# One product of a fast matrix multiplication by seven instead of whole, with sums moved to GpSimd

## The chip, the cores and the metric

The kernel runs on one core of a Trainium2 chip. The core has TensorE (matrix products, called PE in the profile; its loads of the stationary operand are PEld), VectorE (DVE), ScalarE (ACT), GpSimd (POOL) and SyncE (SP), each with a queue of its own that it works off in order. PSUM has eight banks, each of 128 rows of 512 float32 numbers. TensorE adds its results up there, and VectorE and ScalarE read them. The metric is device time in microseconds, and the median of several runs is given.

## What is computed

```python
x = np.random.randn(8, 2048, 2048).astype(np.float32)
w = np.random.randn(2048, 2048).astype(np.float32)
cs = np.cumsum(x, axis=1)
diff = cs - (cs shifted down by one row, with a row of zeros ahead)
out = np.matmul(diff, w)
```

Taking the differences of a running sum gives `x` back, so the kernel computes `x @ w`: 16384 rows by 2048 by 2048, with float32 in and out.

## The kernel before

**Tiles.** The 16384 rows are 128 tiles of 128 rows. The first four tiles are multiplied in the plain way while the weights arrive. The other 124 form 31 groups of four tiles, `g`, `h`, `k`, `l`. Two groups have orders of their own (`group_plain`, `group_half`); the other 29 are objects of the class `Group`. These 29 are nearly all of the run.

**Seven products for eight.** In a group the four tiles and the weights are cut into 2 x 2 blocks, so that a product of blocks in the plain way takes eight block products. A known scheme (Strassen's, in Winograd's form) takes seven, named `P1` to `P7`, at the price of sums of blocks ahead of them (`S1` to `S4` of the tiles, `T1` to `T4` of the weights) and of sums of the results behind them. The same scheme is used once more inside a product: it is then cut into quarters and done in seven quarters `p1` to `p7` of four matmuls each, instead of eight. Before the change `P1` to `P5` are done so. `P6` (S2 x T2) and `P7` (S3 x T3) are done whole, in 2 x 4 steps of four matmuls each (`whole`).

**Steps of a group.** Each step has a name. `load`, `weigh0`, `weigh1`, `scale`, `unit`, `narrow0`, `narrow1`, `turn0`, `turn1` bring in a tile: SP loads both halves into `F` (line 111), ScalarE takes the sum of magnitudes of each half (`weigh`, line 123), VectorE adds the two and takes the reciprocal (`scale`, lines 139 and 141), GpSimd makes the factor that undoes the scaling (`unit`, line 147), ScalarE scales and narrows to float16 in place (`narrow`, line 158), and SP transposes by DMA into the tile's place (`turn`, line 171). The first halves of the tiles take turns in three places of `F`, the second halves in two.
`P1.s1` to `P1.s4` and the like are the small sums of a product by seven (`small_sums`, VectorE, line 544, 128x512 float16); `S1.g` and the like are the sums on whole blocks (line 544, 128x1024). `P1.fp4` and the like are fills: VectorE writes a sum of weights that has no place of its own into the one tile `flow` (line 937), from which the quarter of that name then reads. The quarters' matmuls have line 573, the whole products' line 554.
`by_seven` lets sums of results form in PSUM: ScalarE copies a bank (`cg`, `ct`, line 1023) and VectorE merges banks (`m1`, `m2`, line 1030). `keep.C11g0` scales a bank into a result tile `c` (ScalarE, line 581), `add.C11g0.v` scales another and adds it (VectorE, line 584), `put.C11g0` stores it (SP, line 595). There are seven `c` tiles; a `put` gives its tile back, and the copies `ct` use them too. Banks and the tiles for small sums are handed out and given back in the same way.

**Order.** `ORDER` is a list of all steps of a group, written out. `P1.p2+1` is the step of the group after the current one, `+0` of the current one, `+2` of the one after the next. One round of the list is done for each group. An engine's instructions are issued strictly in the order of the list (`after`), so a step that waits holds up the steps behind it on its engine. Steps that wait for another engine's result are released by semaphores. The last group's `P4` steps follow in `END_ORDER`.

Of the kernel before, what the change touches and what calls it, by code (L numbers as in the profile page):

```python
# [10 lines left out]
def kernel(  # L11
# [6 lines left out]
    nc = tc.nc  # L18
# [113 lines left out]
    def scale_of(t):  # L132
        if t < END:
# [3 lines left out]
            after(  # L137
                "dve",
                lambda: nc.vector.tensor_scalar(m, m2[:, :1], m2[:, 1:2], TINY, ADD, MAX),  # L139
            )  # L140
            after("dve", lambda: nc.vector.reciprocal(s, m))  # L141
            sizes[t] = m

    def unit_of(t):
        if t < END:
            u, m = unit[t], sizes.pop(t)
            after("pool", lambda: nc.gpsimd.tensor_scalar(u, m, uw, None, MUL))  # L147
# [346 lines left out]
    class Inner:  # L494
# [20 lines left out]
        def weights(self):  # L515
# [4 lines left out]
            return {j: pieces_of(t) for j, t in places.items()}  # L520
# [22 lines left out]
    def total(dst, p, q, op):  # L543
        after("dve", lambda: nc.vector.tensor_tensor(dst.all, p.all, q.all, op))  # L544
# [388 lines left out]

    def fill_by(op, a, b):
        def some():
# [4 lines left out]

    sevens = {
# [8 lines left out]
                "p5": fill_by(SUB, quarter_of(1, 1, 1), quarter_of(6, 1, 0)),  # L950
# [5 lines left out]

    class Group:
        def __init__(self, g):
            self.tiles = dict(g=g, h=g + 2, k=g + 1, l=g + 3)
# [26 lines left out]
        def quarter(self, P, j, b, fresh):  # L986
# [4 lines left out]
            def some():  # L991
                to, a = self.bank(b, fresh), self.sums[P][j]
                quarter(
                    to, self.real(a), passed if j in passes else inner.weights()[j], fresh
                )
# [5 lines left out]
        def small_sums(self, P, a, b, dead, places=()):  # L1001
# [5 lines left out]
            def one(j, p, q, op):  # L1007
                if isinstance(to[j], str):
                    self.take(to[j], scratch)
                total(self.real(to[j]), self.real(p), self.real(q), op)  # L1010
# [48 lines left out]
        def add(self, c, b, tag, let=False):  # L1059
            def some():  # L1060
                add(self.at[c], self.at[b], unit[self.row(c)])
# [4 lines left out]
        def put(self, c):  # L1066
            n = 2 * (c[2] == "2") + int(c[4])
            self.step(f"put.{c}", lambda: put(self.at.pop(c), self.row(c), n))

        def plan(self):  # L1070
            tiles = self.tiles
            half = {}
            for c, t in tiles.items():
# [3 lines left out]
                self.step(f"scale.{c}", scale_of, t)  # L1077
# [74 lines left out]
            self.whole("P7", T3, half["g"][0], half["h"][0], *x)  # L1152
# [43 lines left out]
    put.C12g1+0 turn1.h+1 add.C12h1.q+0 P4.p6+0 P4.p5+0 P1.cg+1 P1.p2+1  # L1196
    add.C12h0.q+0 put.C12h0+0 P1.s1+1 narrow1.k+1 P4.s4+0 P4.p3+0 turn0.k+1
    keep.C21g1+0 P1.s2+1 P1.s4+1 P1.p5+1 add.C22h0.x+0 P1.ct+1 add.C21h1.e+0
# [87 lines left out]
```

## Time and profile before

| | |
|---|---|
| median of 3 runs | 1456.87 us (1456.62 to 1457.39) |
| span of the profiled execution | 1455.0 us |
| TensorE busy | 1441.1 us (99%), 6673 matmuls |
| VectorE busy | 1333.3 us (92%) |
| ScalarE busy | 967.5 us (66%) |
| GpSimd busy | 48.6 us (3%) |
| DMA | mean 242 GB/s |

The profiled execution's own time is its span, 1455.0 us from the first to the last instruction; the runs' times have 1.9 us more around it. In the profile's rows "c<-b,of,c" says that a tile c is written from b, of and c; "x26" is a count; "mean ns" is the mean duration of one. In rows in order of time the first number is the start, the second the duration, both in us, and a bracket at the end tells how long the engine had been idle and what ended that. Neighbours on one engine overlap a little, so what an instruction takes from its engine is read from its start to the next one's.

### The profile page before, as it was taken

The page shows a single profiled execution, that of the slowest core. Times are in us where ns is not written, and L with a number is a line of the kernel's source. Part 1 is how long each engine was busy: PE and PEld are TensorE (multiplying, and loading weights), DVE is VectorE, ACT ScalarE, POOL GpSimd, SP SyncE. Part 2 cuts the span into 40 slices and gives each one's busy share as a digit, 9 for nine tenths or more (in the row PEclk, how much of TensorE's full clock was granted, in tenths as well). Part 3 has the DMA queues.
Part 4 walks back from the last instruction along what each step waited for, and adds up shares of the span by engine and source line. Part 5 has one row for each costly group of instructions (what it writes and reads, how often), then busy time and mean ns, then how long its engine had stood idle before and what let it go on. Part 6 is the DMA issues. An engine that isn't in the chain of part 4 may idle for free.

```text
span 1455.0 us, 20120 instructions
## 1 busy us (share of the span) xinstructions
PE 1441.1 (99%) x6673; PEld 652.6 (45%) x6679; DVE 1333.3 (92%) x2302; ACT 967.5 (66%) x1446; POOL 48.6 (3%) x136
## 2 busy tenths in 40 slices
PE   8999999999999999999999999999999999999998
PEld 3444444444444444444444444444444444444443
DVE  7998899999999999999999999999999999999998
ACT  5887656676666666667666667766666766666662
POOL 0111000000000000000000000000000000000000
PEclk9999999999999999999999999999999999999999
DMA  9999868898888998878998888998878898888983
GB/s 360 367 240 299 236 171 234 248 246 232 234 237 237 248 253 230 235 236 233 260 241 233 231 228 240 260 238 241 225 235 247 247 233 239 226 244 246 253 203 123
DMA packets 377752, 351.59 MB, mean 242 GB/s; under 512 B 274800, under 2 KB 274800, under 8 KB 377520
## 3 DMA queue, kind: packets, MB, share of 16 engines
q1 hardware_dynamic: 377088, 348.47, 84.9%
q0 software_dynamic: 560, 1.84, 0.3%
q8 instruction: 52, 0.85, 0.2%
q14 instruction: 52, 0.43, 0.1%
HBM read 150.99 MB, written 134.22 MB: 196 GB/s over the span
## 4 chain that ended last, share of the span: by engine, by line
PE 96%; DMA 2%; DVE 1%; issue 0%; ACT 0%; SPq 0%; DVEq 0%; ACTq 0%
PE b L573 61%; PE b L554 32%; PE b L275 2%; DMA W<-in_w_dram 1%; DMA W<-in_x_dram 1%; DVE c L584 1%; ACT wb L259 0%; PE b L400 0%; DVE x L544 0%; SPq L219 0%; DVE b L1030 0%; DVE flow L937 0%; DVE inner L544 0%; DVE W L541 0%; ACT c L581 0%
## 5 line engine op out<-in xcount | busy, mean ns | idle before, releaser
L584 DVE SCALAR_TENSOR_TENSOR c<-b,of,c 128x512 f32<-128x512 f32 x790 | 574.1, 747 | 74.3 <-PE b L573 64.3
L554 PE MATMUL b<-W,x 128*128 128x512 f16 x2144 | 506.6, 379 | 0.0
L581 ACT ACTIVATE c<-b,of 128x512 f32<-128x512 f32 x492 | 312.6, 680 | 230.9 <-PE b L573 113.3
L573 PE MATMUL b<-W,x 128*128 128x512 f16 x1892 | 452.4, 379 | 0.8 <-ACT b L1023 0.7
L158 ACT ACTIVATE F<-F,of 128x1024 f16<-128x1024 f32 x246 | 282.2, 1147 | 174.8 <-DVE of L141 172.6
L573 PEld LDWEIGHTS <-x 128*128 128x128 f16 x2488 | 243.4, 98 | 295.3 <-issue 2.7
L554 PEld LDWEIGHTS <-x 128*128 128x128 f16 x2144 | 209.8, 98 | 253.0 <-DVE x L544 0.2
L123 ACT ACTIVATE waste<-F 128x1024 uint8<-128x1024 f32 x246 | 259.3, 1054 | 4.6 <-DMA F<-in_x_dram 2.5
L573 PEld LDWEIGHTS <-inner 128*128 128x128 f16 x1648 | 161.2, 98 | 195.6 <-issue 1.3
L573 PE MATMUL b<-W,inner 128*128 128x512 f16 x944 | 242.2, 379 | 0.9 <-DVE b L1030 0.9
L544 DVE TENSOR_TENSOR x<-x,x 128x1024 f16<-128x1024 f16 (+1 forms) x388 | 226.6, 584 | 3.3
L573 PE MATMUL b<-flow,x 128*128 128x512 f16 x588 | 150.9, 379 | 0.0
L573 PE MATMUL b<-inner 128*128 128x512 f16 x472 | 121.1, 379 | 0.0
L937 DVE TENSOR_TENSOR flow<-W 128x2048 f16<-128x2048 f16 x87 | 105.8, 1216 | 0.0
L1030 DVE TENSOR_TENSOR b<-b,c 128x512 f32<-128x512 f32 x116 | 80.6, 695 | 13.9 <-PE b L573 13.9
L147 POOL TENSOR_SCALAR of<-of,uw 128x1 f32<-128x1 f32 x124 | 43.6, 370 | 1306.7 <-DVE of L139 704.1
L937 DVE TENSOR_TENSOR flow<-W,inner 128x2048 f16<-128x2048 f16 x58 | 70.8, 1220 | 0.0
L1023 ACT COPY c<-b 128x512 f32<-128x512 f32 x58 | 33.4, 576 | 51.3 <-PE b L573 51.3
L275 PE MATMUL b<-wb,xP 128*128 128x512 bf16 x234 | 57.0, 395 | 5.3 <-ACT wb L259 3.9
L544 DVE TENSOR_TENSOR inner<-x 128x512 f16<-128x512 f16 x117 | 49.4, 422 | 2.9 <-DMA x<-F 0.9
L1023 ACT COPY b<-b 128x512 f32<-128x512 f32 x87 | 51.2, 588 | 0.5 <-PE b L573 0.5
L544 DVE TENSOR_TENSOR inner<-x,inner 128x512 f16<-128x512 f16 x117 | 49.2, 421 | 2.0
(67 smaller groups left out, 530.0 us busy)
## 6 DMA issues: line engine op xcount, KB each, us to landing
F<-in_x_dram SPq DMA_DIRECT2D x246, 512.0 KB, 5.1
out_dram<-c SPq DMA_DIRECT2D x492, 256.0 KB, 3.0
W<-in_w_dram SPq DMA_DIRECT2D x32, 512.0 KB, 9.6
W<-in_x_dram SPq DMA_DIRECT2D x16, 256.0 KB, 7.2
x<-F SPq DMA_TRANSPOSE x246, 3.4
out_dram<-o POOLq DMA_DIRECT2D x5, 256.0 KB, 4.1
out_dram<-o SPq DMA_DIRECT2D x5, 256.0 KB, 3.5
xP<-in_x_dram SPq DMA_DIRECT2D x1, 1024.0 KB, 5.1
```

The costliest lines, as they stand in the source:

```text
L123: lambda: nc.scalar.activation(waste, where[t][i], ABS, scale=1.0 / ROW, accum_out=sums_of[t][:, i : i + 1],),
L147: after("pool", lambda: nc.gpsimd.tensor_scalar(u, m, uw, None, MUL))
L158: lambda: nc.scalar.activation(narrowed(t)[:, ds(i * NH, NH)], where[t][i], COPY, scale=s),
L275: lambda: nc.tensor.matmul(ps[r][n], xP[:, r, ko, :], wb[h, ko][:, ds(n * NB, NB)], start=(ko == 0), stop=(ko == KO - 1),),
L544: after("dve", lambda: nc.vector.tensor_tensor(dst.all, p.all, q.all, op))
L554: said = nc.tensor.matmul(to[n], a[k], b[k][:, n, :], start=(first and k == 0), stop=(k == KH - 1), skip_group_check=True,)
L573: said = nc.tensor.matmul(to, a[k], b[k], start=(first and k == 0), stop=(k == 3), skip_group_check=True)
L581: after("act", lambda: nc.scalar.activation(c, p, COPY, scale=u))
L584: after("dve", lambda: nc.vector.scalar_tensor_tensor(c, p, u, c, MUL, ADD))
L937: after("dve", lambda: nc.vector.tensor_tensor(in_twos(flow), x, y, op))
L1023: after("act", lambda: nc.scalar.copy(c, p))
L1030: after("dve", lambda: nc.vector.tensor_tensor(t, p, s, ADD))
```

## The change

It consists of these parts.

- `P7` = S3 x T3 is done in seven quarters in every `Group`, by a new method `onto`. It adds onto four banks that already hold sums: ScalarE copies partial results of two more banks `q` and `e` into `c` tiles (`c1`, `c5`, `c6`, `c7`), and VectorE merges them into the four (`a1`, `a5g`, `a5h`, `a6`, `a7h`, `a7k`). Three of the seven sums of weights come by fills (`fp4`, `fp5`, `fp7`); the quarters of T3 are changed once, ahead of the first group, by two sums.
- From the eleventh tile on, the first halves in `F` take turns in two places. The third holds a sum of weights for `P5`, which so loses the fill `fp5`.
- Nine small sums (`ON_POOL`) and the sum ahead of each reciprocal go to GpSimd. The reciprocal becomes a step `recip`.
- Eight of the sixteen results (`LATE`) are kept by a plain copy and added up without a factor. A step `last` on ScalarE then scales the result in its tile. The last group does as before.
- The order is a new one; each step of the list above that stands in the old order, and is not replaced, stands in the new one, most at another place.

```diff
+    THREE = 11
     for i, t in enumerate(queue_of_x):
-        where[t] = [F[:, i % 3, :], F[:, 3 + i % 2, :]]
+        j = i % 3 if i < THREE else (i - THREE) % 2
+        where[t] = [F[:, j, :], F[:, 3 + i % 2, :]]
...
+    ON_POOL = "P1.s2 P2.s2 P2.s4 P3.s1 P3.s4 P4.s2 P4.s4 P5.s3 P5.s4".split()
+    def total(dst, p, q, op, pool=False):
+        if pool:
+            after("pool", lambda: nc.gpsimd.tensor_tensor(dst.all, p.all, q.all, op))
+        else:
+            after("dve", lambda: nc.vector.tensor_tensor(dst.all, p.all, q.all, op))
...
+    in_5.Q1 = F[:, 2, :].bitcast(f16).rearrange("p (k n) -> p k n", k=4)
+    in_7 = Inner(5, None, quarter_of(5, 0, 1), None)
...
-                "p5": fill_by(SUB, quarter_of(1, 1, 1), quarter_of(6, 1, 0)),
+        "P7": (
+            in_7,
+            {
+                "p4": fill_by(SUB, quarter_of(5, 1, 0), quarter_of(5, 0, 1)),
+                "p5": fill_by(SUB, quarter_of(5, 1, 1), quarter_of(5, 0, 1)),
+                "p7": fill_by(SUB, quarter_of(5, 0, 1), quarter_of(5, 0, 0)),
+            },
+        ),
...
+    LATE = 'C12g0 C12g1 C12h1 C12h0 C11g1 C11h1 C21g1 C21h1'.split()
+            self.late = LATE if g + 4 < END else ()
...
+        def onto(self, P, h0, h1, g0, g1):
+            q, e = f"{P}q", f"{P}e"
+            def snap(name, b, let=False):
+                def some():
+                    c, p = self.take(name, free), self.at[b]
+                    after("act", lambda: nc.scalar.copy(c, p))
+                    self.close(b, let)
+                return some
+            self.quarter(P, "p1", q, True)
+            self.step(f"{P}.c1", snap(f"{P}1", q))
+            self.merge(f"{P}.a1", g0, g0, f"{P}1", let=True)
+            self.quarter(P, "p2", g0, False)
+            self.quarter(P, "p5", e, True)
+            self.step(f"{P}.c5", snap(f"{P}5", e, True))
+            self.merge(f"{P}.a5g", g1, g1, f"{P}5")
+            self.merge(f"{P}.a5h", h1, h1, f"{P}5", let=True)
+            self.quarter(P, "p3", g1, False)
+            self.quarter(P, "p6", q, False)
+            self.step(f"{P}.c6", snap(f"{P}6", q))
+            self.merge(f"{P}.a6", g1, g1, f"{P}6", let=True)
+            self.quarter(P, "p7", q, False)
+            self.step(f"{P}.c7", snap(f"{P}7", q, True))
+            self.merge(f"{P}.a7h", h1, h1, f"{P}7")
+            self.merge(f"{P}.a7k", h0, h0, f"{P}7", let=True)
+            self.quarter(P, "p4", h0, False)
...
             def some():
-                keep(self.take(c, free), self.at[b], unit[self.row(c)])
+                to, p, u = self.take(c, free), self.at[b], unit[self.row(c)]
+                if c in self.late:
+                    after("act", lambda: nc.scalar.copy(to, p))
+                else:
+                    keep(to, p, u)
...
+                if c in self.late:
+                    after("dve", lambda: nc.vector.tensor_tensor(to, p, to, ADD))
+                else:
+                    add(to, p, u)
...
+            if c in self.late:
+                self.step(f"last.{c}", lambda: keep(self.at[c], self.at[c], unit[self.row(c)]))
...
-            self.whole("P7", T3, half["g"][0], half["h"][0], *x)
+            self.small_sums("P7", A("g", 0), A("h", 0), True)
+            self.onto("P7", *x)
```

Of the new order, these are the stretches that the prediction speaks of. They begin a round, go on in its middle, and end it:

```diff
+    weigh0.g+1 add.C11h0.q+0 S4.h+0 P5.s2+0 P5.s3+0 P6h.1+0 P6h.2+0 put.C21g1-1
+    keep.C12g1+0 weigh1.g+1 S3.h+0 P7.s1+0 P7.s2+0 P4.s1+0 P7.p1+0 P7.c1+0 P4.p1+0
+    P7.s3+0 scale.g+1 P7.p5+0 put.C11g1+0 P7.a1+0 keep.C12h1+0 P7.s4+0 recip.g+1 P7.p6+0
+    P7.fp7+0 P7.c5+0 P7.p2+0 add.C22g0.x+0 load.h+1 P5.s4+0 P7.c6+0 narrow0.g+1 P7.a5g+0
+    P7.a5h+0 P5.p5+0 P7.a6+0 P7.p7+0 P4.p2+0 weigh1.h+1 P5.p6+0 P3.s1+0 P3.s3+0
+    keep.C21g0+0 P7.p3+0 P7.c7+0 add.C21g0.x+0 put.C11h0+0 P3.p1+0 P3.s2+0 P5.ct+0
+    P5.m1+0 P7.a7h+0 narrow1.g+1 weigh0.h+1 unit.g+1 turn0.g+1 P3.s4+0 scale.h+1
+    unit.h+1 add.C12g0.q+0 P5.p3+0 P5.fp4+0 P5.p7+0 unit.l+0 put.C22g0+0 last.C12g0+0
+    keep.C22g1+0 P5.m2+0 P3.p6+0 add.C22g1.x+0 P3.p3+0 add.C12g1.q+0 P5.p4+0 recip.h+1
+    P4.s2+0 put.C21g0+0 keep.C12h0+0 P4.p6+0 P3.p7+0 keep.C22h1+0 P7.a7k+0 P7.fp4+0
+    add.C12h1.z+0 turn1.g+1 P4.s4+0 keep.C22h0+0 P3.p4+0 put.C22g1+0 add.C22h1.x+0
...
+    put.C12h0+0 P1.s2+1 put.C22h0+0 P1.p2+1 P4.p7+0 add.C21g1.x+0 add.C21h1.e+0 P4.fp4+0
...
+    keep.C21h0+0 P1.m1+1 P1.s3+1 P1.p7+1 P2.s1+1 P1.fp4+1 P1.m2+1 P2.s2+1 unit.k+1
+    P2.s4+1 add.C21h0.x+0 add.C11g0.v+1 P1.p3+1 narrow1.k+1 weigh0.l+1 keep.C11h1+1
...
+    P6g.2+1 P2.p4+1 last.C12g1+0 add.C11g1.e+1 S4.g+1 P3.fp2+1 put.C11g0+1 turn0.l+1
+    turn1.l+1 S1.h+1 S2.h+1 P5.p2+1 last.C11h1+1 keep.C11h0+1 put.C11h1+1 keep.C22g0+1
+    put.C21h1+0 P6g.3+1 P6g.0+1 P3.p2+1 load.g+2 P6h.3+1 keep.C12g0+1 S3.g+1 put.C12g1+0
+    last.C11g1+1 P5.s1+1 P7.fp5+1 add.C12g0.z+1 last.C21g1+0 P6h.0+1
```

More of the change, by code (lines that the diff above doesn't have):

```diff
@@ L519, in weights @@
             )
-            return {j: pieces_of(t) for j, t in places.items()}
+            return {j: pieces_of(t) for j, t in places.items() if t is not None}
     passed = [flow[:, k, :] for k in range(4)]
@@ new lines @@
+    add.C21g1.q+0 add.C22h0.x+0 put.C22h1+0 last.C12h0+0 P1.cg+1 P1.s1+1 last.C12h1+0
+    put.C12h0+0 P1.s2+1 put.C22h0+0 P1.p2+1 P4.p7+0 add.C21g1.x+0 add.C21h1.e+0 P4.fp4+0
+    P1.p5+1 weigh1.k+1 weigh0.k+1 P2.cv+1 P1.s4+1 keep.C11g0+1 scale.k+1 recip.k+1
+    P1.ct+1 put.C12h1+0 P1.p6+1 load.l+1 add.C21h1.q+0 P4.p4+0 P2.p2+1 narrow0.k+1
+    keep.C21h0+0 P1.m1+1 P1.s3+1 P1.p7+1 P2.s1+1 P1.fp4+1 P1.m2+1 P2.s2+1 unit.k+1
+    P2.s4+1 add.C21h0.x+0 add.C11g0.v+1 P1.p3+1 narrow1.k+1 weigh0.l+1 keep.C11h1+1
```

81 lines of the change are left out of this document (38 added, 43 removed).

## The prediction

> **What bounds the kernel now.** I read the page first, then one steady group as a window, then that group's VectorE in order of time, then ScalarE, GpSimd and the tail.
>
> ```profile
> span 1455.0 us, 20120 instructions
> PE 1441.1 (99%) x6673; PEld 652.6 (45%) x6679; DVE 1333.3 (92%) x2302; ACT 967.5 (66%) x1446; POOL 48.6 (3%) x136
> ```
> ```profile
> core 0: us, PE busy (x) PEld busy (x) DVE busy (x) ACT busy (x) POOL busy (x), PEclk, DMA share, GB/s
> 703.80:747.83 44.03, 44.03 (x206) 19.98 (x205) 40.78 (x73) 29.61 (x46) 1.07 (x4) 1.00 0.84 228
> ```
> ```profile
> L937 DVE TENSOR_TENSOR flow<-W,S 128x2048 f16<-128x2048 f16 x29 | 35.3, 1219 | 0.0
> ```
>
> The last row is P1's fill, one in each group: 29 groups of the written order. The window runs from one of them to the next. TensorE is busy for all 44.03 us at clock 1.00, so it sets the pace. By the code a group has 204 matmuls (35 quarters and 16 steps of four; the 206 counts two that reach over an edge), hence 44.03 / 204 = 0.2158 us for each. VectorE is next, at 40.78 us of 44.03. Its own pace is read from start to start, as durations of neighbours overlap:
>
> ```profile
> 702.54 0.75 DVE L584 SCALAR_TENSOR_TENSOR c<-b,of,c 128x512 f32<-128x512 f32 x1
> 703.21 0.69 DVE L1030 TENSOR_TENSOR b<-b,c 128x512 f32<-128x512 f32 x1
> 703.80 1.22 DVE L937 TENSOR_TENSOR flow<-W,S 128x2048 f16<-128x2048 f16 x1
> 704.93 0.42 DVE L544 TENSOR_TENSOR inner<-x 128x512 f16<-128x512 f16 x1
> 705.39 0.42 DVE L544 TENSOR_TENSOR inner<-inner,x 128x512 f16<-128x512 f16 x1
> 705.73 0.69 DVE L1030 TENSOR_TENSOR b<-b,c 128x512 f32<-128x512 f32 x1
> 706.33 0.41 DVE L544 TENSOR_TENSOR inner<-x,inner 128x512 f16<-128x512 f16 x1
> 706.67 1.41 DVE L544 TENSOR_TENSOR x<-x,x 128x1024 f16<-128x1024 f16 x2
> 708.00 0.74 DVE L584 SCALAR_TENSOR_TENSOR c<-b,of,c 128x512 f32<-128x512 f32 x1
> 708.66 0.20 DVE L139 TENSOR_SCALAR of<-of 128x1 f32<-128x1 f32 x1
> 708.89 0.16 DVE L141 RECIPROCAL of<-of 128x1 f32<-128x1 f32 x1
> 709.00 0.75 DVE L584 SCALAR_TENSOR_TENSOR c<-b,of,c 128x512 f32<-128x512 f32 x1
> ```
>
> Scaled add 0.66 (708.00 to 708.66), merge 0.60, fill 1.13, small sum 0.34, or 0.46 where the next one needs it (704.93 to 705.39). Two S sums take 1.33: 0.60 free, 0.73 where the second needs the first (here it does). The sum ahead of the reciprocal 0.23, the reciprocal 0.11. Before, a group has 26 adds, 20 small sums, 8 S sums, 6 fills, 4 merges, 4 scales: 17.2 + 6.8 + 4.8 + 6.8 + 2.4 + 1.4 = 39.4 us. The other 4.6 us are neighbours that need each other, and waits for TensorE:
>
> ```profile
> DVE c L584 <- PE b L573: 2.1, 5, 0.7
> DVE b L1030 <- PE b L573: 0.5, 1, 0.5
> ```
>
> **The change part by part, per group.**
>
> *TensorE.* S3 x T3 goes from 32 matmuls to 28: 200 x 0.2158 = 43.17 us, a gain of 0.863. It lies wholly on the path, as TensorE has no idle time here.
>
> *VectorE, added.* Six merges, 6 x 0.60 = 3.6. P7's four small sums, 4 x 0.34 = 1.36, and 0.12 more for s2, which needs s1 just ahead. Three fills for P7, less P5's p5 fill, which gets a place of its own: 2 x 1.13 = 2.26. *Taken away.* Nine small sums, 9 x 0.34 = 3.06. Four sums ahead of a reciprocal, 4 x 0.23 = 0.92. Eighteen adds lose their scale; a plain add from PSUM into SBUF is not in the trace, its nearest rows are the merge (0.60) and the scaled add (0.66); it is the merge's operation with another place for its output, so 0.60: 18 x 0.06 = 1.1, or nothing at the other end. Net +2.3: 41.7 us. To this come waits that the order itself shows: P3's fill stands right behind the quarter that reads the last one (P2.p4), 0.6, P7's p4 fill behind P5.p4, 0.2, and some 0.2 for S1 before S2. VectorE needs 42.7 us, against TensorE's 43.17. Its spare time falls from 4.6 us to 0.5: this is the first thing to see here.
>
> *GpSimd.* Its only rows in a group are these:
>
> ```profile
> 709.03 0.53 POOL L147 TENSOR_SCALAR of<-of,uw 128x1 f32<-128x1 f32 x2 [21.75 <-DVE of L139]
> 730.77 0.54 POOL L147 TENSOR_SCALAR of<-of,uw 128x1 f32<-128x1 f32 x2 [21.21 <-DVE of L141]
> ```
>
> 0.27 us for one number in each row of the tile; the sum ahead of the reciprocal takes about as much, and each `recip` now also waits for it in VectorE's queue, while `narrow` waits in ScalarE's. A 128x512 sum on GpSimd is not in the trace. From below: 0.27 fixed and no more than VectorE's 0.34 less its overhead, some 0.5. From above: 0.27 and VectorE's 0.60 for as many f32 elements, some 0.9. GpSimd has 43 us for nine of them and eight small ones, so its own time costs nothing by either; what counts is what it does to VectorE. Both GpSimd rows lie beside a scaled add, which reads one operand from PSUM (709.00); no row shows GpSimd beside a VectorE sum with both operands in SBUF. So the cost to VectorE lies between nothing and the whole length of all nine, 9 x 0.9 = 8.1 us. I read it from what the order puts behind each: P5.s3, P3.s4, P4.s2, P4.s4, P1.s2, P2.s2 and P2.s4 have two or three PSUM readers (1.2 to 1.9 us) on VectorE beside them; P5.s4 and P3.s1 run on behind each other where P7.s4 and the fill P7.fp7 stand. I take 0.5 us, about one of these two: VectorE 43.2.
>
> The Trainium skill, "SBUF — State Buffer", section "Who interferes with whom", says that a VectorE instruction with two SBUF inputs and a GpSimd instruction that reads SBUF exclude each other, whichever starts first. The rows above neither show nor deny it. "GPSIMD Engine Reference", section 3.1, has 4497 ns for a GpSimd tensor_tensor of 2048 fp32 elements, by which I estimate 1.1 us for 512. By the two, the seven stay covered, and the other two cost 0.6 to 1.7 us: VectorE at 43.3 to 44.4, and the end at about 1446 (with the coupling below) to 1470.
>
> *ScalarE.* Starts apart give its pace:
>
> ```profile
> 722.02 0.56 ACT L1023 COPY c<-b 128x512 f32<-128x512 f32 x1
> 722.49 0.69 ACT L581 ACTIVATE c<-b,of 128x512 f32<-128x512 f32 x1
> 723.07 1.05 ACT L123 ACTIVATE waste<-F 128x1024 uint8<-128x1024 f32 x1
> 734.04 1.05 ACT L123 ACTIVATE waste<-F 128x1024 uint8<-128x1024 f32 x1
> 735.08 1.14 ACT L158 ACTIVATE F<-F,of 128x1024 f16<-128x1024 f32 x1
> 740.95 1.15 ACT L158 ACTIVATE F<-F,of 128x1024 f16<-128x1024 f32 x1
> 741.99 0.60 ACT L1023 COPY b<-b 128x512 f32<-128x512 f32 x1
> ```
>
> Copy 0.47, scaled keep 0.58, weigh 1.04, narrow 1.04. Added: four copies of P7, 1.9; eight late scalings from SBUF to SBUF (not in the trace; between half a narrow, 0.52, and a keep, 0.58), 4.6; eight keeps become copies, -0.9. With 8 weighs, 8 narrows, 16 keeps and 5 copies (28.3) ScalarE gets to 33.9 of 43.2 us. It has room; but the bank q of P7 goes p1, copy, p6, copy, p7, copy, each copy behind other work in ScalarE's queue with TensorE's next quarter waiting for it. The order has one quarter (0.86 us) or more between: I cost it at nothing, and 0.3 us where weigh1.g ahead of the first copy is late.
>
> *Loads.* F's first halves turn over among two places, not three.
>
> ```profile
> F<-in_x_dram SPq DMA_DIRECT2D x246, 512.0 KB, 5.1
> out_dram<-c SPq DMA_DIRECT2D x492, 256.0 KB, 3.0
> x<-F SPq DMA_TRANSPOSE x246, 3.4
> ```
>
> A place is held for load 5.1, two weighs 2.1, sums 0.5, two narrows 2.1, two turns about 1.3 + 3.4: 14.5 us, of 2 x 43.17 / 4 = 21.6. No new transfer is issued. SP's queue gets no longer, but loads stand behind `put`s that wait for a late scaling; 7 us of room cover that. A place of c is now taken 22 times a group (18 before) out of seven, some 13.7 us from take to take; a put's 3.0 us fits.
>
> *Coupling.* With TensorE at 43.17 and VectorE at 43.2, every late reader shows. Before, 2.6 us of VectorE's waits cost TensorE nothing, as VectorE caught up in its spare time. I take 0.25 us a group (from 0 to 1): 43.42.
>
> *Tail and head.* The new order leaves the last group 108 matmuls (23.3 us) in its last round, with VectorE's 7 + 13 adds at 0.66, 9 small sums, 8 merges, 4 fills, 2 S sums: 13.2 + 3.0 + 4.8 + 4.5 + 1.2 = 26.7 us and no other work to mix in: +3.4. Before it left 20 matmuls:
>
> ```profile
> 1442.34 6.37 PE L573 MATMUL b<-W,x 128*128 128x512 f16 x28
> 1448.55 1.03 PE L573 MATMUL b<-flow,x 128*128 128x512 f16 x4
> 1446.23 4.04 DVE L584 SCALAR_TENSOR_TENSOR c<-b,of,c 128x512 f32<-128x512 f32 x6
> ```
>
> and TensorE hardly waited. Three sums over weights (3 x 1.13) are added once, in the first round, where the order has 92 matmuls (19.9 us) against 15.4 us of VectorE: nothing.
>
> *Sum.* 28 distances x (43.42 - 44.03) = -17.1; the last group -0.9 + 3.4 = +2.5; together -14.6. The profiled span is 1455.0, the median of the runs 1456.87, so 1.9 us lie around the span and stay: 1442.3 us. A change under 0.2% (2.9 us) can't be told from none.
>
> **The rivals.**
>
> *Gain nearly eaten (1447 to 1454).* VectorE becomes the bound at 43.6 to 43.85 us: 28 x -0.43 to -0.18, and +2.5. For it: 0.5 us of spare time, and the two sums on GpSimd that nothing covers. Against: the room that a plain add may leave.
>
> *Slower: GpSimd holds VectorE up.* If each of the nine keeps a VectorE sum waiting for half its length, 0.25 to 0.45 us, VectorE needs 42.7 + 2.3 to 4.1 = 45.0 to 46.8: 28 x +0.97 to +2.8, and +2.5: 1487 to 1538, and about 1473 where only the uncovered two do so, each for its full 0.9 (44.5). It decides from 42.7 + 1.3, when VectorE passes 43.95 and the tail uses up the rest. For it: 31 of VectorE's 71 instructions have both operands in SBUF, and VectorE has no spare time. Against: the order of seven of the nine. The skill's rule above speaks for this one.
>
> *Slower: a late load or scaling.* ScalarE waits for load.g at the head of a round, and the first copy of P7, then TensorE, with it. load.g lies behind put.C11h1, which needs last.C11h1, on ScalarE. 1.5 us a group beyond the forecast: 28 x +0.9 and +2.5, 1484; from 0.5 us it eats the gain. Against: 7 us of room for a place of F.
>
> *The gain whole.* No coupling and no collisions: 28 x -0.863, and -0.9 to +2.5: 1432 to 1435.
>
> **How the numbers follow.** Forecast with the whole gain, 1432 to 1447, likeliest 1442.3: 0.42. Gain nearly eaten: 0.14. No change, 1454 to 1460: 0.05. GpSimd: 0.27. Late load: 0.12. So faster 0.56, same 0.05, slower 0.39. The range from 1433 to 1480 leaves out some 0.03 below and 0.15 above, where GpSimd's upper prices lie; the likeliest case's own is 1432 to 1447.
>
> **What would show it.** Distance between P1's fills: 43.2 to 43.6 by the forecast, over 44.1 by the slower ones. VectorE's waits for TensorE fall from 2.6 us to under 1.5, its rows come close to filling the window. Plain adds 0.60 apart. GpSimd rows of 128x512: 0.5 to 0.9 us. TensorE's idle time ended by VectorE (fills, P7's merges) speaks for GpSimd's collisions, ended by ScalarE's copies for a late load; a gap ahead of VectorE's SBUF sums that no semaphore ends, while GpSimd runs, shows the collision itself. The prediction is wrong if GpSimd's sums take well over 1 us, or a plain add more than a scaled one.

## The result and the profile after

The changed kernel takes 1500.12 us (median of four runs, 1497.73 to 1503.25), the kernel before 1456.84 beside it. The ratio is 1.0298, with a 95% interval from 1.0282 to 1.0313: slower by 3%. The forecast was 1442.3 us, with a range up to 1480. Direction and range were both wrong.

The span, busy times and the chain of work that ended last, by engine; first the changed kernel, then the chain of the kernel before:

```profile
span 1500.3 us, 21260 instructions
PE 1442.9 (96%) x6563; PEld 634.9 (42%) x6563; DVE 1405.8 (94%) x2280; ACT 1154.3 (77%) x1786; POOL 520.0 (35%) x509
...
PE 41%; DVE 28%; DMA 16%; issue 6%; ACT 6%; SPq 2%; POOL 0%; ACTq 0%; DVEq 0%
```
```profile
PE 96%; DMA 2%; DVE 1%; issue 0%; ACT 0%; SPq 0%; DVEq 0%; ACTq 0%
```

Before, the chain was TensorE nearly from end to end. After, TensorE holds 41% of it and has 57 us of idle time; the rest goes to and fro between VectorE, ScalarE and transfers. No engine is busy all the time. GpSimd, with ten times its work of before, has 0% of the chain; but a VectorE row that GpSimd holds up counts there as VectorE's.

Where the time came from is read from window rows, from the third of P1's fills to the 28th, 25 whole groups (columns as in the prediction's window: length, busy time of PE, PEld, DVE, ACT, POOL, then clock, share of the DMA engines, GB/s). Before:

```profile
263.50:1364.24 1100.74, 1100.74 (x5102) 499.03 (x5101) 1019.65 (x1801) 740.24 (x1126) 26.73 (x100) 1.00 0.86 239
```

After, the same 25 groups, and one ordinary group alone:

```profile
272.77:1406.85 1134.08, 1100.47 (x5001) 483.11 (x5000) 1076.67 (x1776) 904.82 (x1427) 435.10 (x425) 1.00 0.87 232
...
862.51:907.04 44.53, 43.73 (x201) 19.40 (x200) 43.15 (x73) 36.27 (x59) 17.12 (x17) 1.00 0.89 236
```

A group took 44.03 us and now takes 1134.08 / 25 = 45.36. Before, all distances between these fills lay from 44.02 to 44.04. Now they run from 43.47 to 47.74: this is a kernel that waits now here, now there. TensorE is busy for as long as before, 1100.47 us, with four matmuls fewer in each group; 200 matmuls at the 0.2158 us of before would fill 43.17 us, and the rows take 44.02. So part of its waiting stands in rows that count as busy. The 45.3 us between the spans are 25 x 1.33 = 33.3 in these groups, 9.3 ahead of the third fill (272.77 against 263.50), and 2.6 behind the 28th (1500.3 - 1406.85 = 93.4, against 90.8).

What ends the idle times of ScalarE, VectorE and TensorE in the changed kernel (us in total, times, longest), and then, for the first row, the same wait in the kernel before:

```profile
ACT waste L125 <- DMA F<-in_x_dram: 77.2, 67, 3.1
ACT c L1116 <- DVE c L603: 41.2, 28, 1.6
ACT c L1116 <- DMA out_dram<-c: 23.8, 20, 3.3
DVE c L603 <- ACT c L600: 24.2, 27, 2.4
DVE x L563 <- DMA x<-F: 13.4, 18, 1.9
PE b L592 <- DVE c L1127: 17.6, 29, 2.2
PE b L592 <- ACT c L1086: 9.0, 19, 1.8
```
```profile
ACT waste L123 <- DMA F<-in_x_dram: 2.5, 2, 2.3
```

ScalarE stands 77.2 / 29 = 2.7 us a group ahead of `weigh`, until a load has landed; the kernel before had two such waits in its whole run. Two more kinds of transfer appear: a copy into a `c` tile that waits for the store which still reads it, and an S sum that waits for a turned tile. Behind ScalarE's waits stand its keeps, and the adds that need them (`DVE c L603 <- ACT c L600`). TensorE's largest row, `PE b L592 <- DVE c L1127`, comes about once in a group and has another source, which is shown below.

The transfers themselves (count, KB, median us from issue to landing) answer to the three rows of before, 5.1, 3.0 and 3.4:

```profile
F<-in_x_dram SPq DMA_DIRECT2D x246, 512.0 KB, 5.8
out_dram<-c SPq DMA_DIRECT2D x492, 256.0 KB, 3.2
x<-F SPq DMA_TRANSPOSE x246, 3.3
```

The medians move little, the spread more. Between 400 and 1350 us a load took 5.1 us on average before, with a tenth of them above 5.8; after it is 6.0, and a tenth above 7.5. For stores the slowest tenth went from 4.9 to 6.8.

Against that stands the lead, from the issue of a tile's load to the start of the first `weigh` that reads it. A load of `g` before, and one after, in order of time:

```profile
704.22 0.90 SPq L111 DMA_DIRECT2D F<-in_x_dram  x2
...
713.04 1.06 ACT L123 ACTIVATE waste<-F 128x1024 uint8<-128x1024 f32 x1
```
```profile
872.62 0.89 SPq L113 DMA_DIRECT2D F<-in_x_dram  x2
...
874.93 1.33 ACT L600 ACTIVATE c<-c,of 128x512 f32<-128x512 f32 x2
878.00 1.06 ACT L125 ACTIVATE waste<-F 128x1024 uint8<-128x1024 f32 x1 [1.74 <-DMA F<-in_x_dram]
```

Before, the load has 8.8 us, more than it needs. After it has 5.4, of which ScalarE spends the last 1.74 waiting. Between 400 and 1350 us the leads of `g`, `h`, `k`, `l` were 8.6, 9.9, 9.2 and 9.0 us on average; they are 5.3, 8.2, 8.1 and 5.2 now, the waits included. Without the wait ScalarE would come to `g` 3.9 us after the issue, and the half that it reads first lands after 5.3; to `h` it would come after 7.1, and there it reads the second half first, which is down after 8.1. So `g` waits in 19 of 21 groups and `h` in all 21, while `k` never does. The lateness belongs to two loads at their places in the order; it isn't chance.

GpSimd's sums do collide with VectorE's, at one place above all. In order of time, the fill `P7.fp4` beside `P4.s4`:

```profile
848.77 1.15 POOL L561 TENSOR_TENSOR x<-x,x 128x512 f16<-128x512 f16 x1 [0.43 <-PE b L592]
848.85 2.16 DVE L958 TENSOR_TENSOR flow<-W 128x2048 f16<-128x2048 f16 x1
850.93 0.68 DVE L1127 TENSOR_TENSOR c<-b,c 128x512 f32<-128x512 f32 x1
851.53 0.74 DVE L603 SCALAR_TENSOR_TENSOR c<-b,of,c 128x512 f32<-128x512 f32 x1
```

The fill takes 2.16 us where it takes 1.22 alone. Summed over the fills this is 0.91 us a group. TensorE's next quarter waits 0.57 us for the adds behind this fill: that is its row of 17.6 us above. So there are two suspects, transfers that come late and GpSimd, and the experiments take them apart.

### The profile page after: what moved, and what is told of

Same layout as the page of the kernel before. It is cut to its first block, busy times and chain, and to the rows that moved or that the text cites. A ratio compares the mean times of both kernels' runs of the same rounds, so it can differ in the third digit from the quotient of the medians.

```text
span 1500.3 us, 21260 instructions
## 1 busy us (share of the span) xinstructions
PE 1442.9 (96%) x6563; PEld 634.9 (42%) x6563; DVE 1405.8 (94%) x2280; ACT 1154.3 (77%) x1786; POOL 520.0 (35%) x509
## 4 chain that ended last, share of the span: by engine, by line
PE 41%; DVE 28%; DMA 16%; issue 6%; ACT 6%; SPq 2%; POOL 0%; ACTq 0%; DVEq 0%
PE b L592 28%; PE b L573 10%; DVE flow L958 8%; DMA F<-in_x_dram 7%; DVE b L1061 6%; DMA out_dram<-c 6%; DVE c L1127 6%; DVE c L603 4%; PE b L289 3%; DMA x<-F 2%; ACT c L600 2%; DVE x L563 2%; DVE inner L563 1%; SPq L614 1%; ACT waste L125 1%
## 5 line engine op out<-in xcount | busy, mean ns | idle before, releaser
L592 PE MATMUL b<-W,x 128*128 128x512 f16 x2124 | 508.3, 379 | 28.1 <-DVE c L1127 17.0
L592 PEld LDWEIGHTS <-x 128*128 128x128 f16 x2952 | 286.8, 98 | 389.6 <-issue 43.0
L1127 DVE TENSOR_TENSOR c<-b,c 128x512 f32<-128x512 f32 x504 | 325.1, 679 | 2.1 <-ACT c L1116 1.6
L125 ACT ACTIVATE waste<-F 128x1024 uint8<-128x1024 f32 x246 | 259.6, 1055 | 78.7 <-DMA F<-in_x_dram 77.2
L592 PEld LDWEIGHTS <-inner 128*128 128x128 f16 x1996 | 191.7, 98 | 268.0 <-DVE inner L563 25.2
L592 PE MATMUL b<-W,inner 128*128 128x512 f16 x1176 | 289.0, 380 | 9.1 <-DVE b L1061 4.8
L573 PE MATMUL b<-W,x 128*128 128x512 f16 x1216 | 278.0, 379 | 4.1 <-DVE x L563 4.1
L603 DVE SCALAR_TENSOR_TENSOR c<-b,of,c 128x512 f32<-128x512 f32 x286 | 207.8, 742 | 30.4 <-ACT c L600 24.2
L600 ACT ACTIVATE c<-b,of 128x512 f32<-128x512 f32 x268 | 180.2, 679 | 72.1 <-issue 26.6
L561 POOL TENSOR_TENSOR x<-x,x 128x512 f16<-128x512 f16 x87 | 128.9, 1482 | 274.1 <-DVE inner L563 258.4
L592 PE MATMUL b<-flow,x 128*128 128x512 f16 x820 | 210.3, 379 | 0.2
L958 DVE TENSOR_TENSOR flow<-W 128x2048 f16<-128x2048 f16 x145 | 201.9, 1392 | 0.1
L1061 DVE TENSOR_TENSOR b<-b,c 128x512 f32<-128x512 f32 x290 | 192.3, 691 | 4.8 <-ACT c L1086 3.4
L561 POOL TENSOR_TENSOR inner<-x,inner 128x512 f16<-128x512 f16 x87 | 125.6, 1443 | 121.2 <-DVE inner L563 69.8
L600 ACT ACTIVATE c<-c,of 128x512 f32<-128x512 f32 x224 | 155.9, 718 | 1.1 <-DVE c L1127 1.1
L142 POOL TENSOR_SCALAR of<-of 128x1 f32<-128x1 f32 x112 | 96.4, 861 | 123.6 <-ACT waste L125 123.6
L592 PE MATMUL b<-inner 128*128 128x512 f16 x472 | 116.4, 379 | 0.0
```

The costliest lines, as they stand in the source:

```text
L125: lambda: nc.scalar.activation(waste, where[t][i], ABS, scale=1.0 / ROW, accum_out=sums_of[t][:, i : i + 1],),
L561: after("pool", lambda: nc.gpsimd.tensor_tensor(dst.all, p.all, q.all, op))
L573: said = nc.tensor.matmul(to[n], a[k], b[k][:, n, :], start=(first and k == 0), stop=(k == KH - 1), skip_group_check=True,)
L592: said = nc.tensor.matmul(to, a[k], b[k], start=(first and k == 0), stop=(k == 3), skip_group_check=True)
L600: after("act", lambda: nc.scalar.activation(c, p, COPY, scale=u))
L603: after("dve", lambda: nc.vector.scalar_tensor_tensor(c, p, u, c, MUL, ADD))
```

## The experiments

Two theories. **T, transfers:** the new order uses places, turned tiles and `c` tiles about when their transfers land, and waits where they land late. **G, GpSimd:** its sums take VectorE's time, which has none to spare, and what is late is late because of that. In the diffs, `move(name, ahead, at)` takes a step out of `ORDER` and puts it ahead of another; a fourth number tells to which group the step then belongs. All were compared with the kernel before on the same chips (1456.6 us). The table gathers time, ratio with its interval, and the mean distance between fills over the same 25 groups (in f3 the first of them still has full stores).

| run | from | us | ratio to before (95%) | us a group |
|---|---|---|---|---|
| the change | | 1500.1 | 1.030 (1.028 to 1.031) | 45.36 |
| e1_short_sums | after | 1475.2 | 1.013 (1.011 to 1.015) | 44.41 |
| e5_fp4_later | after | 1492.7 | 1.024 (1.023 to 1.026) | 44.97 |
| e4_before_pool | before | 1486.8 | 1.021 (1.019 to 1.022) | 45.01 |
| e2_early_loads | after | 1573.2 | 1.079 (1.077 to 1.081) | 48.18 |
| e3_short_early | after | 1569.7 | 1.077 (1.076 to 1.079) | 48.07 |
| e7_before_two | before | 1826.0 | 1.251 (1.247 to 1.255) | 57.5 |
| e8_short_three | after | 1753.5 | 1.203 (1.202 to 1.205) | 54.4 |
| e9_three | after | 1785.4 | 1.226 (1.224 to 1.228) | 55.5 |
| f1_light_loads | after | 1451.1 | 0.997 (0.995 to 0.998) | 43.48 |
| f2_light_short | after | 1446.9 | 0.993 (0.992 to 0.995) | 43.41 |
| f3_light_puts | after | 1454.9 | 0.999 (0.998 to 0.999) | 43.62 |
| f4_no_late | after | 1486.0 | 1.020 (1.019 to 1.022) | 44.79 |
| g4_before_light | before | 1456.4 | 1.000 (0.999 to 1.001) | 44.03 |
| g1_act_loads | after | 1601.0 | 1.099 (1.095 to 1.103) | 49.3 |
| g2_act_loads_all | after | 1617.5 | 1.111 (1.109 to 1.113) | 49.7 |
| g3_no_late_fp4 | after | 1737.7 | 1.193 (1.191 to 1.195) | 53.9 |

**GpSimd's part, by shortening its sums.**

```diff
-  nc.gpsimd.tensor_tensor(dst.all, p.all, q.all, op)
+  nc.gpsimd.tensor_tensor(dst.all[:, :32], p.all[:, :32], q.all[:, :32], op)
```

> The changed kernel with its nine GpSimd sums cut to 32 of 512 columns (the rest of each sum is left out). G, GpSimd holds VectorE up: the 0.9 us a group by which VectorE's fills are stretched goes, and 0.3 us of waiting for GpSimd; 45.4 to about 44.2 us a group, 1465 us or less. L, loads come late because F has two places: ScalarE still waits some 2.7 us a group for loads, and the time stays over 1485 us.

25 of the 43 us go. ScalarE's wait for loads stays as it was:

```profile
ACT waste L125 <- DMA F<-in_x_dram: 73.8, 67, 2.8
```

The fills no longer stretch (under 0.01 us a group), and TensorE's wait for the add behind one falls from 17.6 to 2.0 us. But 44.41 us a group is still above 44.03. Both theories have a part so far.

**The one collision taken away.** `P7.fp4` goes to a place where no sum of GpSimd runs, and `P7.p4` with it.

```diff
+    move("P7.fp4", 0, ("put.C12g0", 0))
+    move("P7.p4", 0, ("add.C12h1.q", 0))
```

> The changed kernel with the fill P7.fp4 moved behind add.C12h1.z and add.C22h1.x, and P7.p4 behind P3.p5, so that the fill no longer starts beside GpSimd's P4.s4. G, and this one meeting is what the GpSimd sums cost: fills are stretched by under 0.2 us a group, and the time comes to that of the short sums, 1470 to 1480 us. If the cost lies in other meetings as well, over 1485 us.

The stretch is gone (under 0.01 us a group), but only 7.5 us with it, where 29 x 0.91 = 26 us of stretch went. ScalarE's wait for loads grows instead, from 77.2 to 82.7 us, and all waits of ScalarE and VectorE for loads of x, stores and turns from 129 to 144 us: much of what the collision cost comes back as a wait for transfers.

**The nine sums alone, in the order of before.**

```diff
+    ON_POOL = "P1.s2 P2.s2 P2.s4 P3.s1 P3.s4 P4.s2 P4.s4 P5.s3 P5.s4".split()
...
+            after("pool", lambda: nc.gpsimd.tensor_tensor(dst.all, p.all, q.all, op))
```

> The kernel before, with its own order, and only the nine small sums moved to GpSimd. VectorE has 4.6 us of room there. G: fills next to a GpSimd sum are stretched, a GpSimd sum takes 1.15 us or more, but VectorE still has room after giving up 3 us of sums: within 0.5% of before, 1450 to 1465 us. If the order's quarters wait for the slow sums instead, over 1465 us. L says nothing here.

Slower by 30 us, and every group alike. A group of GpSimd's rows (busy, mean ns, idle before and what ended it), and a row of VectorE's waits, name the price:

```profile
L547 POOL TENSOR_TENSOR inner<-inner,x 128x512 f16<-128x512 f16 x58 | 67.1, 1156 | 281.7 <-DVE inner L549 160.7 <-PE b L578 115.6 <-DMA out_dram<-c 5.4
```
```profile
DVE inner L549 <- POOL inner L547: 79.4, 58, 1.7
```

The old order needs each sum at once, and a sum of 1.16 us stands where one of 0.34 stood: VectorE waits 79.4 / 29 = 2.7 us a group for results. Here it is mainly the length of the sum that costs; the fills are stretched by only 0.3 us a group. In the changed kernel VectorE has no such wait of note: the new order puts the sums earlier.

**Loads earlier.**

```diff
+    move("load.g", 2, ("turn0.l", 1))
+    move("load.h", 1, ("put.C12g1", 0), 2)
```

> The changed kernel with load.g moved ahead of turn0.l and load.h ahead of put.C12g1, some 4 to 5 us earlier in SP's queue. L: ScalarE's waits for loads fall from 2.7 us a group to under 1, VectorE's waits for ScalarE and for turned tiles from 1.6 to under 0.6, and the time to 1460 to 1475 us. G: the fills stay stretched by 0.9 us a group and the time stays over 1490 us.

The waits for loads vanish (0.14 us a group), and the kernel loses 73 us more. What ScalarE and VectorE wait for now:

```profile
ACT c L1116 <- DMA out_dram<-c: 114.2, 29, 6.0
...
DVE x L563 <- DMA x<-F: 99.5, 31, 5.5
```

`turn0.l`, now behind 1 MB of loads, lands 7.0 us after its issue instead of 3.3, and the stores behind `load.h` come late in the same way. A transfer that is moved forward makes the next ones late. With short sums besides:

> Both edits together: short GpSimd sums and the earlier loads. If G and L are the whole of it, a group takes 43.2 to 43.6 us and the kernel 1437 to 1450 us. If VectorE and TensorE are too full to go together even so (C), it stays over 1455 us.

Only 3.5 us less. In this order GpSimd's sums cost next to nothing (in e2, with full sums, the fills stretch by 0.01 us a group); so G's price is not fixed.

**Transfers made light, no step moved.** This run, with f2 behind it, tells T from G. From the 24th tile on, a load brings in a quarter of the columns; the engines do all their work.

```diff
-  where[t][i], x2[ds(t * P, P), ds(i * NH, NH)]
+  where[t][i][:, : NH // 4 if t >= PLAIN + 20 else NH],
+  x2[ds(t * P, P), ds(i * NH, NH // 4 if t >= PLAIN + 20 else NH)],
```

> The changed kernel with the loads of x from the 24th tile on cut to a quarter of their columns (the rest of each load is left out), no step moved. D, transfers land too late for an order that uses F's places and the c tiles again at once: loads land in 4 us or less, not 5.8, ScalarE's 2.7 us a group of waits for loads go, and a group takes 44.2 to 44.5 us, 1466 to 1477 us, what is left being GpSimd's. C, VectorE is too full: over 1490 us.

With GpSimd's sums in full, 49 us go, more than the change had lost. The window over the same 25 groups; the chain by engine and the loads, from the page; and ScalarE's wait for loads:

```profile
272.13:1359.16 1087.03, 1082.12 (x5000) 487.52 (x4999) 1055.85 (x1777) 899.90 (x1426) 457.98 (x425) 1.00 0.63 170
```
```profile
PE 81%; DVE 7%; DMA 6%; ACT 3%; issue 2%; POOL 1%; SPq 0%; DVEq 0%; ACTq 0%
...
F<-in_x_dram SPq DMA_DIRECT2D x208, 128.0 KB, 2.9
```
```profile
ACT waste L126 <- DMA F<-in_x_dram: 6.8, 6, 3.4
```

43.48 us a group, many of them 43.2: TensorE is the bound again, as forecast. GpSimd is even busier than in the change (457.98 against 435.10), yet the fills stretch by 0.04 us a group instead of 0.91. The two steps haven't been kept apart: `P7.fp4` and `P4.s4` still meet in each of these groups. One meeting in f1:

```profile
867.34 1.23 DVE L959 TENSOR_TENSOR flow<-W 128x2048 f16<-128x2048 f16 x1
867.45 2.13 POOL L562 TENSOR_TENSOR x<-x,x 128x512 f16<-128x512 f16 x1 [0.67 <-PE b L593]
```

Now the fill starts first, by 0.11 us, and it is GpSimd's sum that is held up, which costs VectorE nothing. In the change GpSimd starts first, by 0.07 us, in 24 of the 25 groups; the one group where the fill does took 43.47 us, the shortest of all. In f1 GpSimd starts first in one group alone, and that one took 45.95 us, the longest. (In f2 below, with short sums, the same group still takes 45.25, so it was late for another reason.) The light loads have turned round the order of two starts, and the collision's price has gone with it.

> Light loads and short GpSimd sums together (the rest of both is left out). If D and G make up the whole loss, 43.2 to 43.5 us a group and 1437 to 1447 us, a gain over the kernel before. If VectorE's fullness costs by itself (C), over 1455 us.

With light loads, shorter sums bring 4 us; with full loads (e1) they brought 25. The two causes don't simply add up. A group takes 45.36 us with both, 44.41 without GpSimd's long sums, 43.48 without full loads, 43.41 without either. Late loads alone cost 44.41 - 43.41 = 1.00, GpSimd's long sums alone 43.48 - 43.41 = 0.07, and the remaining 0.88 arise only where both are there. The stores instead of the loads:

```diff
-  after("sp", lambda: nc.sync.dma_start(out2[ds(t * P, P), ds(at * NB, NB)], c))
+  n = NB // 4 if t >= PLAIN + 20 else NB
+  after("sp", lambda: nc.sync.dma_start(out2[ds(t * P, P), ds(at * NB, n)], c[:, :n]))
```

> The changed kernel with the stores of the results from the 24th tile on cut to a quarter of their columns (the rest of each store is left out), loads in full. D by way of the c tiles: ScalarE's 1.4 us a group of waits for stores go, loads behind them land sooner too, 1470 to 1485 us. D by way of F's places alone: over 1490 us.

45 us go, nearly as many, though each load is as large as before; ScalarE's waits for loads halve (1.3 us a group). So it isn't one kind of transfer: loads and stores together leave too little slack in this order. The fills stretch by 0.08 us a group here, so this gain, too, contains that of the collision.

The control: the kernel before, with the same light loads.

> The kernel before with the loads of x from the 24th tile on cut to a quarter of their columns (the rest of each load is left out). D says that the kernel before had room for its transfers: TensorE stays at 44.03 us a group, 1455 to 1458 us. If light loads speed up any kernel, 1450 us or less.

44.03 us a group, no change. Light loads don't speed up the kernel before, which doesn't wait for them.

**Late scaling undone.** All sixteen results are scaled as they are added, as before.

```diff
-    LATE = 'C12g0 C12g1 C12h1 C12h0 C11g1 C11h1 C21g1 C21h1'.split()
+    LATE = ()
```

> The changed kernel with no late scaling: all results are scaled as they are kept and added, as before; no step named last. ScalarE has 3.8 us a group less to do, VectorE 18 x 0.06 = 1.1 us more. C: 1.1 us a group slower, 1525 us or more. If ScalarE's queue, with the stores behind it, holds the rest up: faster, 1470 to 1490 us.

14 us faster, although VectorE gets 1.1 us more work a group (18 adds at 0.66 instead of 0.60). If VectorE's fullness were the bound, this would be slower. The loads don't come sooner, though: ScalarE waits 88.3 us for them, against 77.2. What falls is the stretch of the fills, from 0.91 to 0.17 us a group, more than the 45.36 - 44.79 = 0.57 that a group gains. So this gain can be the collision's, and that late scaling kept the loads back isn't shown.

**A different queue for the loads.** ScalarE issues them (`load_by_act` is `load` on its queue), at places meant to be 1 to 3 us earlier.

```diff
-  lambda t=t: (load(t, 0), load(t, 1))
+  lambda t=t: (load_by_act(t, 0), load_by_act(t, 1))
...
+    move("load.g", 2, ("P5.cg", 1))
+    move("load.h", 1, ("last.C11g1", 1), 2)
+    move("load.k", 1, ("keep.C22h0", 0))
+    move("load.l", 1, ("weigh0.k", 1))
```

> The changed kernel with the loads of x issued from ScalarE's queue in place of SP's, at places of ScalarE's order where the turn that they wait for has landed (1 to 3 us earlier than now). Q, loads are late because they stand behind stores and turns in SP's queue, and hold those up: ScalarE's waits for loads and stores fall under 1.5 us a group (4.1 now), 1465 to 1480 us. B, the DMA engines are simply too busy to land them sooner: landing stays at 5.8 us or more, no gain, 1490 us or more.

100 us slower than the change. The transfers, and ScalarE's first wait:

```profile
out_dram<-c SPq DMA_DIRECT2D x492, 256.0 KB, 3.8
F<-in_x_dram ACTq DMA_DIRECT2D x222, 512.0 KB, 6.0
```
```profile
ACT c L1125 <- DMA out_dram<-c: 152.9, 48, 6.4
```

In a queue of their own the loads land no sooner (6.0 us), and the stores, with no load ahead of them in SP's queue, land later than before (3.8 for 3.2). This is what one pool of engines would show. The Trainium skill, "DMA: Bandwidth & Descriptors", section "Issuing engines are not separate DMA queues", says that transfers run on the same 16 DMA engines and interleave, whichever engine starts them; the run agrees. As the place changed along with the queue, the run alone doesn't prove it.

**Attempts at a better order.** g2 joins g1, f4 and e5; g3 joins f4 and e5, and puts `load.g` and `load.l` ahead of one store each.

> Loads from ScalarE's queue, no late scaling, and P7.fp4 behind two adds: the three edits that ought to help, together. Q: 1450 to 1465 us. B: 1475 us or more.

> No late scaling, P7.fp4 behind two adds, load.g ahead of put.C11h1 and load.l ahead of put.C22h0, all in SP's queue as now. If a load that is 1 us sooner helps more than the stores behind it lose: 1465 to 1480 us; if not, 1482 us or more.

Both lose far more. In g3 the two stores that were passed cost ScalarE 287 us of waits:

```profile
ACT c L600 <- DMA out_dram<-c: 286.8, 61, 8.4
```

**Two or three places of F.** e7 gives the kernel before two places, with two loads moved so far back that the place is free. e8 and e9 give the changed kernel its third place back (so P5's fill `fp5` returns), with the loads moved up right behind the turns; e8 has short sums, too.

```diff
-        j = i % 3 if i < THREE else (i - THREE) % 2
+        j = i % 3
...
+    ORDER.insert(ORDER.index(("P3.s3", 0)), ("P5.fp5", 0))
+    move("P5.p5", 0, ("P7.c7", 0))
+    move("load.k", 1, ("P4.s4", 0))
+    move("load.l", 1, ("add.C12g1.e", 0))
+    move("load.g", 2, ("P2.s3", 1))
+    move("load.h", 1, ("S1.h", 1), 2)
```

> The kernel before with two places in F for the first halves from the eleventh tile on, load.k moved behind turn1.g and load.l behind turn1.h, and nothing else. L, the places alone cost: waits for loads on ScalarE over 1 us a group, and over 1470 us. If two places only hurt where VectorE and ScalarE have no room, under 1462 us.

> The changed kernel with short GpSimd sums (the rest of each is left out), three places in F again, each load right behind the turn that precedes its old place's reuse, and P5's p5 by a fill, which is 1.13 us more for VectorE. L, lateness from two places is what the short sums left over: in spite of the added fill 43.5 to 44.0 us a group, 1446 to 1460 us, under the 1475 of the short sums alone. C, VectorE is simply full: a fill more makes it slower, 1490 us or more.

> The same with the GpSimd sums in full: the changed kernel with three places, the earlier loads and the fill. L: 44.5 to 45 us a group, 1475 to 1488 us, in spite of the fill. C: 1515 us or more. G adds 20 to 28 us to the kernel with the short sums in either case.

All missed, by T and by G alike. In e7 ScalarE waits 308 us for loads; in e9 the loads are in time and the stores pay (the first row is e7's, the others e9's):

```profile
ACT waste L125 <- DMA F<-in_x_dram: 308.3, 80, 9.3
```
```profile
ACT c L1116 <- DMA out_dram<-c: 226.8, 54, 6.6
```
```profile
out_dram<-c SPq DMA_DIRECT2D x492, 256.0 KB, 6.2
```

A store behind a load lands after 6.2 us instead of 3.2. These runs give no price for the two places by themselves, as each moved loads too. They repeat e2's lesson at a greater size.

## Why the prediction was wrong, point by point

**The step that failed** is the one on loads: "A place is held for load 5.1, two weighs 2.1 [...]: 14.5 us, of 21.6", so that "7 us of room cover that"; and beside it "a put's 3.0 us fits". It added up how long a place is in use and compared this with how often one is wanted. That shows that two places can suffice. It doesn't show that the order issues each load early enough. The number to take was the lead: 8.6 to 9.9 us before, when every load was in time. In the new order ScalarE comes to `g` after 3.9 us and to `h` after 7.1, while their loads need 5.3 and 8.1; that makes most of the 77.2 us of waits. And it took one median for all loads, 5.1, where `h`'s load, issued 4.5 us behind `g`'s (877.15 behind 872.62), takes 7.6 for its second half. Where the forecast had nothing, late loads cost 1.00 us a group by themselves (e1 against f2), and 45.36 - 43.48 = 1.88 with all GpSimd work in place (f1). That the waits then hold up stores, and these the next loads, is argued from the queues; f3 fits it, as light stores halve the waits for loads.

**The second step that failed** is the choice of the 0.5 us for collisions. The prediction named `P4.s4` among the sums that readers of PSUM cover, but in the order the fill `P7.fp4` stands only two steps ahead of `P4.s4`. They meet, and with late loads GpSimd's sums cost 45.36 - 44.41 = 0.95 us a group, of which 0.88 arises only together with the late loads.

**The rival that came true** was the late load or scaling, given 0.12. Of its mechanism the late load is right, with `load.g` at the head of a round, though it didn't name `h`. That late scaling delays it isn't shown: without that scaling, in f4, `g` waits longer, 2.6 us a group against 1.4. Its 1.5 us a group lie between the 1.00 and the 1.88 that late loads cost; it had nothing for the head. The "7 us of room" that stood against it were the same error again.

**GpSimd holding VectorE up**, given 0.27, came true in part. Its 1487 to 1538 us hold the measured 1500 by luck: it had each of the nine sums keep VectorE waiting, 2.3 to 4.1 us a group. One sum did it, and the price isn't fixed: 0.95 us a group where transfers are late, 0.07 where they are in time.

At the two sums that I had called uncovered VectorE lost nothing: `P5.s4` does meet `P7.fp7` in every group, but the fill starts first, and GpSimd's sum takes about 2 us instead. The figure of 0.5 to 0.9 us for a sum was too low: alone it takes 1.15 (below). That did little harm by itself, GpSimd being busy 17 of 44.5 us. Of the two GpSimd rows of before that I had put beside a scaled add, the one at 730.77 lies beside one only at its end, which changes nothing here. The sign that was to tell the two rivals apart, what ends TensorE's idle time, pointed at GpSimd first (17.6 us behind the fill, 9.0 behind ScalarE's copies); it took the experiments to see the loads.

**TensorE** was right: 200 matmuls, and groups of 43.2 us once transfers are light. **Coupling** of 0.25 agrees with f2 by luck: 43.41 - 43.17 = 0.24 on average there, but most groups take 43.2 and a few up to 45.25, so it isn't a price that every group pays. **VectorE** was right: summed row by row its work rose from 44.9 to 48.1 us a group (neighbours overlap, so the sum exceeds the busy time), by 2.3 without the 0.91 of stretched fills, for 2.3 forecast. The plain add at 0.60 was right: 850.93 to 851.53 in the rows above. A full VectorE by itself wasn't the cause of the loss: f1 has all its work, 1055.85 / 25 = 42.2 us busy, in 43.48. **ScalarE**: its busy time rose from 740.24 / 25 = 29.6 to 904.82 / 25 = 36.2 us, by 6.6 for 5.6 forecast; the room was there, but not at the times when it was wanted.

**The tail** was priced too high: behind the last fill, the 29th, the kernel takes 47.7 us for 46.7, so +0.9 for -0.9 + 3.4. (The 2.6 us behind the 28th hold one more distance between fills, 45.7 for 44.0.) **The head** was wrong: I had put it at nothing. Of the 9.3 us ahead of the third fill 0.8 lie ahead of the first, 6.9 between the first and the second, and 1.5 in the next distance, which is an ordinary late one. Four sums over weights stand within 10 us of the first group (one of them was there before), and TensorE runs dry behind them. VectorE's rows of these sums in order of time, and the same time as windows of 5 us:

```profile
189.01 1.22 DVE L555 TENSOR_TENSOR F<-W 128x2048 f16<-128x2048 f16 x1
...
190.48 3.31 DVE L555 TENSOR_TENSOR W<-W 128x2048 f16<-128x2048 f16 x2
...
197.24 1.22 DVE L555 TENSOR_TENSOR W<-W 128x2048 f16<-128x2048 f16 x1
```

```profile
190.00:195.00 5.00, 3.55 (x17) 1.50 (x16) 4.86 (x5) 3.03 (x7) 3.28 (x2) 1.00 0.75 252
195.00:200.00 5.00, 1.45 (x6) 0.45 (x6) 4.93 (x10) 0.00 (x0) 0.00 (x0) 0.81 0.17 65
200.00:205.00 5.00, 5.00 (x14) 1.80 (x13) 2.96 (x7) 2.38 (x4) 1.15 (x1) 0.51 0.00 0
205.00:210.00 5.00, 5.00 (x25) 2.28 (x24) 5.00 (x9) 3.91 (x7) 2.08 (x3) 1.00 0.55 156
```

VectorE is full, TensorE idle for 1.45 + 3.55 = 5.0 us, and then it runs at half its clock: 14 matmuls in 5 us where 23 fit, 2 us more. That is most of the 6.9 us by which the first distance between fills, 50.9 us, exceeds the 44.0 of before. Comparing totals for the round (19.9 us of matmuls, 15.4 of VectorE) could not show that these sums stand in one place.

**What stays open.** Whether an order exists that keeps the gain with full transfers; the orders tried with loads elsewhere (e2, e9, g1, g2, g3) all lost. What the two places cost by themselves. How much of f1's gain is the loads' own landing and how much is what they leave to other transfers; f3 says only that light stores relieve the loads. What turns round the two starts at `P7.fp4` in one group and not in another. No version was found that beats the kernel before without leaving work out.

## What to carry to other kernels

When a change shortens the period of an order written out by hand, list for each transfer its lead (from issue to first use, by the new order) beside the landing of that transfer at its own place in the queue, not one median for all beside the sum of holding times. Where the DMA engines are as busy as here (0.86 and 0.87 of the time), moving one transfer forward took from those behind it in every run that tried, so look at all queues together. Where a GpSimd sum and a VectorE sum meet, ask which starts first: a difference of 0.2 us decided here whether VectorE lost 0.94 us. To learn whether transfers are what a kernel waits for, make them lighter without moving a step, and do the same to the kernel before as a control.

## What the runs showed of the hardware

GpSimd's sums and VectorE's collisions, as groups of rows of the changed kernel (busy, mean ns | idle before):

```profile
L561 POOL TENSOR_TENSOR inner<-x 128x512 f16<-128x512 f16 x29 | 33.4, 1150 | 1.6 <-PE b L592 1.5
L561 POOL TENSOR_TENSOR x<-x,x 128x512 f16<-128x512 f16 x87 | 128.9, 1482 | 274.1 <-DVE inner L563 258.4
L1127 DVE TENSOR_TENSOR c<-b,c 128x512 f32<-128x512 f32 x504 | 325.1, 679 | 2.1 <-ACT c L1116 1.6
```

A GpSimd sum of 128x512 float16 takes 1.15 us, and 1.9 to 2.1 where a VectorE sum that reads both operands from SBUF is already running. Such a VectorE sum is held up in the same way: 2.16 us for a fill of 1.22 that starts 0.08 us behind a GpSimd sum of 1.15. The one that starts first isn't held up: in f1 the same fill starts 0.11 us ahead and takes 1.23, and the sum 2.13. VectorE's adds that read one operand from PSUM keep their 0.68 us beside GpSimd: none of the 504 takes over 0.70. This is the rule of the Trainium skill, "SBUF — State Buffer", section "Who interferes with whom", which the prediction weighed and which the rows of before couldn't show: the trace agrees. The figure of the Trainium skill, "GPSIMD Engine Reference", section 3.1, by which I had estimated 1.1 us for the sum, was nearer than my bounds from VectorE's rows. The other surprise is the clock in the rows of the head: 0.51 for about 5 us behind a stretch in which TensorE was busy only 1.45 of 5 us. The 5 us without matmuls cost 2 us more by the slow clock behind them.
